# Moving the stores of a routing kernel from the sync engine's DMA queue to ScalarE's, almost a pair late

## The chip, the cores and the metric

The kernel runs on one core of one Trainium2 chip. The metric is device time in microseconds (us), lower is better. The core has a matrix engine (PE, with its weight loads listed apart as PEld), VectorE (DVE), ScalarE (ACT), GpSimd (POOL) and a sync engine (SP) that here does nothing but issue DMA transfers. A run's own median is quoted, and its ratio to the kernel before is the mean of its runs over the mean of the runs of the kernel before in the same rounds, so it is not quite the ratio of the two medians.

## The reference, cut to what matters

```python
B, S, D, H = 64, 1024, 1024, 16            # all fp32
best_head = np.argmax(x @ route_w, axis=-1)             # one head per token
for h in range(H):                                      # x split in 16 heads of 64
    out[:, :, h, :] = (x_heads[:, :, h, :] @ experts[h]) * (best_head == h)[:, :, None]
```

There are 65,536 tokens of 4 KB: 268 MB are read and 268 MB are written. The kernel works in tiles of 128 tokens, and in pairs of tiles: 256 pairs, each with 1 MB in and 1 MB out.

## The kernel before: the parts that matter

```python
WAYS = 2;  XIN_BUFS = 10;  OUT_BUFS = 6;  AHEAD = 7
ORDER = "TTTTFTFTFTTFTFTFTTTTTT"      # T: a transpose of the next pair, F: a whole block of this one

def load(g):                                           # one pair: two transfers of 512 KB
    xin = xin_pool.tile([P, 2, D], FP32, ...)
    for r in range(WAYS):
        nc.sync.dma_start(out=xin[r::WAYS], in_=xg[g, r::WAYS])      # 8 KB a partition
    return xin
...
def split_pass(xt):                                    # 20 small matmuls a tile, 64x64 weights
    for p in range(NS):
        for half in range(2):
            for th in range(2):
                nc.tensor.matmul(ps[...], lhsT=xt[...64 x 64...], rhs=mv[...64 x 80...], ...)
    nc.scalar.copy(out=raw[...], in_=ps[...])
...
for j in range(-2 * AHEAD, NT + 2, 2):                 # j: first tile of a pair
    if j + 2 * AHEAD < NT:
        xins[j + 2 * AHEAD] = load(j // 2 + AHEAD)
    ...
    for i in pair:                                     # the pair that was transposed last time
        work[i] = split_pass(xts[i])                   # a burst of 40 small matmuls (80 in the trace)
    for step in order:                                 # T: transpose (ScalarE copies every fourth)
        ...                                            # F: whole block; after three, finish()
        if f % NF == 0:                                # finish(): argmax, mask, products into ot
            finish(ot[:, i % 2, :], ps_w, *work.pop(i))
            if i == pair[1]:
                for r in range(WAYS):
                    nc.sync.dma_start(out=og[i // 2, r::WAYS], in_=ot[r::WAYS])
```

Loads and stores share one queue and stand in it in program order: two loads, two stores, two loads. In the trace a transfer is never issued before the one eight places earlier has landed (0.02 us after that landing at the earliest), so at most eight are in flight, and eight are in flight for 95% of the time.

## Time and profile before

| | |
|---|---|
| time, median of 3 | 1344.7 us (1339.88 to 1344.74) |
| profiled run, span | 1338.1 us |
| pair of tiles when nothing disturbs it | 4.93 us on PE |
| 256 such pairs | 1261 us |
| DMA busy share, 20 to 1300 us | 1.01 |

The page of the profile, cut to its span, busy times, DMA rows (40 equal slices: busy tenths, then GB/s), the data queue, the chain that ended last, and the DMA issues (KB each, median us from issue to landing):

```profile
span 1338.1 us, 66342 instructions
...
PE 1290.3 (96%) x27648; PEld 1208.3 (90%) x27648; DVE 933.7 (70%) x4098; ACT 923.2 (69%) x1537; POOL 721.9 (54%) x1031
...
DMA  8999999999999999999999999999999999999997
GB/s 340 421 421 416 413 407 409 407 407 406 412 398 377 418 417 399 395 412 414 398 393 404 410 416 418 402 408 397 410 407 410 412 407 417 416 405 416 417 409 327
...
q1 hardware_dynamic: 81920, 536.94, 98.6%
...
DMA 96%; PE 1%; SPq 0%; DVE 0%; issue 0%; POOL 0%; ACT 0%; ACTq 0%; POOLq 0%; DVEq 0%
DMA out_dram<-ot 95%; DMA xin<-in_x_dram 1%; SPq L106 0%; PE ps_w L150 0%; PE ps_t L115 0%; DMA mv<-in_route_w_dram 0%; PE ps_s L136 0%; POOL ot L181 0%; DVE ot L173 0%; ACTq L88 0%; ACT raw L143 0%; ACT xt L117 0%; DVE mask L164 0%; POOLq L249 0%; DVE lg L158 0%
...
xin<-in_x_dram SPq DMA_DIRECT2D x512, 512.0 KB, 10.2
out_dram<-ot SPq DMA_DIRECT2D x512, 512.0 KB, 10.2
```

Three things are to be seen. The DMA engines are full from the second slice to the last but one. The chain that ended last is stores. And a transfer lands 10.2 us after it is issued, because eight of 512 KB are nearly always in flight (4.2 MB at 408 GB/s are 10.3 us).

The waits list of the compute engines (who waited for whom: us in total, times, longest), cut to what touches DMA and PE:

```profile
DVE ot L173 <- DMA out_dram<-ot: 83.8, 104, 1.8
...
POOL ot L181 <- DMA out_dram<-ot: 76.3, 40, 3.0
...
PEld ps_s L136 <- issue: 62.8, 241, 1.9
...
PE ps_s L136 <- issue: 21.9, 35, 1.8
...
PE ps_t L115 <- DMA xin<-in_x_dram: 6.9, 2, 6.6
```

DVE and POOL wait 84 and 76 us for an output buffer that a store still reads.

From these views the kernel before is bound by the DMA engines, and the compute is held back through the output buffers.

### The profile page before, as it was taken

The page shows a single profiled execution, that of the slowest core. Times are in us where ns is not written, and L with a number is a line of the kernel's source. Part 1 is how long each engine was busy: PE and PEld are TensorE (multiplying, and loading weights), DVE is VectorE, ACT ScalarE, POOL GpSimd, SP SyncE. Part 2 cuts the span into 40 slices and gives each one's busy share as a digit, 9 for nine tenths or more (in the row PEclk, how much of TensorE's full clock was granted, in tenths as well). Part 3 has the DMA queues.
Part 4 walks back from the last instruction along what each step waited for, and adds up shares of the span by engine and source line. Part 5 has one row for each costly group of instructions (what it writes and reads, how often), then busy time and mean ns, then how long its engine had stood idle before and what let it go on. Part 6 is the DMA issues. An engine that isn't in the chain of part 4 may idle for free.

```text
span 1338.1 us, 66342 instructions
## 1 busy us (share of the span) xinstructions
PE 1290.3 (96%) x27648; PEld 1208.3 (90%) x27648; DVE 933.7 (70%) x4098; ACT 923.2 (69%) x1537; POOL 721.9 (54%) x1031
## 2 busy tenths in 40 slices
PE   7999999999999999999999999999999999999995
PEld 7888998999998999999998999889998999999995
DVE  4666766677776777777777677667777777767775
ACT  5666766767766777777676776667766767767673
POOL 3455555555555555555555555555555555555554
PEclk9999999999999999999999999999999999999998
DMA  8999999999999999999999999999999999999997
GB/s 340 421 421 416 413 407 409 407 407 406 412 398 377 418 417 399 395 412 414 398 393 404 410 416 418 402 408 397 410 407 410 412 407 417 416 405 416 417 409 327
DMA packets 84412, 541.51 MB, mean 405 GB/s; under 512 B 18576, under 2 KB 18576, under 8 KB 18576
## 3 DMA queue, kind: packets, MB, share of 16 engines
q1 hardware_dynamic: 81920, 536.94, 98.6%
q8 instruction: 218, 3.57, 1.0%
q10 hardware_dynamic: 2192, 0.33, 0.1%
q14 instruction: 82, 0.67, 0.1%
HBM read 268.76 MB, written 268.44 MB: 401 GB/s over the span
## 4 chain that ended last, share of the span: by engine, by line
DMA 96%; PE 1%; SPq 0%; DVE 0%; issue 0%; POOL 0%; ACT 0%; ACTq 0%; POOLq 0%; DVEq 0%
DMA out_dram<-ot 95%; DMA xin<-in_x_dram 1%; SPq L106 0%; PE ps_w L150 0%; PE ps_t L115 0%; DMA mv<-in_route_w_dram 0%; PE ps_s L136 0%; POOL ot L181 0%; DVE ot L173 0%; ACTq L88 0%; ACT raw L143 0%; ACT xt L117 0%; DVE mask L164 0%; POOLq L249 0%; DVE lg L158 0%
## 5 line engine op out<-in xcount | busy, mean ns | idle before, releaser
L181 POOL TENSOR_TENSOR ot<-raw,mask 128x384 f32<-128x384 f32 (+1 forms) x1024 | 721.2, 725 | 605.6 <-ACT xt L117 338.0
L117 ACT COPY xt<-ps_t 128x512 f32<-128x512 f32 x1024 | 576.7, 589 | 288.5 <-PE ps_t L115 288.0
L115 PE MATMUL ps_t<-ident,xin 128*128 128x128 f32 x4096 | 756.5, 277 | 9.7 <-DMA xin<-in_x_dram 6.9
L150 PE MATMUL ps_w<-mf,xt 128*128 128x144 f32 x3072 | 580.3, 289 | 1.5 <-DVE ot L173 1.1
L115 PEld LDWEIGHTS ps_t<-ident,xin 128*128 128x128 f32 x4096 | 499.7, 141 | 33.6 <-issue 8.9
L150 PEld LDWEIGHTS ps_w<-mf,xt 128*128 128x128 f32 x3072 | 464.2, 191 | 8.8 <-DVE ot L173 6.3
L136 PE MATMUL ps_s<-mv,xt 64*64 64x80 f32 x20480 | 430.0, 232 | 22.6 <-issue 21.9
L136 PEld LDWEIGHTS ps_s<-mv,xt 64*64 64x64 f32 x20480 | 381.1, 133 | 73.2 <-issue 62.8
L143 ACT COPY raw<-ps_s 128x704 f32<-128x704 f32 x512 | 371.1, 747 | 104.3 <-PE ps_s L136 64.9
L173 DVE TENSOR_TENSOR ot<-ps_w,mask 128x384 f32<-128x384 f32 x512 | 285.6, 558 | 98.5 <-DMA out_dram<-ot 83.8
L127 DVE TENSOR_REDUCE lgs<-ps_s 128x16 f32<-128x96 f32 x512 | 121.4, 251 | 106.3 <-ACT raw L143 105.4
L164 DVE TENSOR_SCALAR mask<-hid,ix 128x16 f32<-128x16 f32 x512 | 120.0, 234 | 56.0 <-POOL ot L181 0.9
L124 DVE TENSOR_REDUCE lgw<-ps_w 128x16 f32<-128x48 f32 x512 | 103.3, 202 | 78.9 <-PE ps_w L150 78.1
L158 DVE TENSOR_TENSOR lg<-lgs,lgw 128x16 f32<-128x16 f32 x512 | 131.8, 257 | 17.6
L160 DVE MAX8 mx<-lg 128x8 f32<-128x16 f32 x512 | 91.2, 178 | 17.6
L162 DVE FIND_INDEX8 ix<-mx,lg 128x8 uint32<-128x16 f32 x512 | 86.5, 169 | 0.0
L162 DVE MATCH_VALUE_LOAD ix<-mx,lg 128x8 f32 x512 | 47.2, 92 | 17.7
L117 ACT ACT_TABLE_LOAD x1 | 1.3, 1283 | 7.3 <-DMA mf<-in_experts_dram 7.3
L81 DVE MEMSET mf<- 128x432 f32 x1 | 0.4, 418 | 0.9 <-PEq L238 0.9
masks.py:197 POOL MEMSET ident<- 128x128 f32 x1 | 0.2, 205 | 0.3 <-POOLq L238 0.3
masks.py:199 POOL TENSOR_SCALAR_AFFINE_SELECT ident<-ident 128x128 f32<-128x128 f32 x1 | 0.3, 294 | 0.0
L238 POOL MEMSET const-float32-0.0<- 128x1 f32 x1 | 0.1, 99 | 0.2 <-issue 0.2
(5 smaller groups left out, 0.6 us busy)
## 6 DMA issues: line engine op xcount, KB each, us to landing
xin<-in_x_dram SPq DMA_DIRECT2D x512, 512.0 KB, 10.2
out_dram<-ot SPq DMA_DIRECT2D x512, 512.0 KB, 10.2
mv<-in_experts_dram ACTq DMA_DIRECT2D x2, 48.0 KB, 4.7
mf<-in_experts_dram ACTq DMA_DIRECT2D x2, 48.0 KB, 2.4
mv<-in_experts_dram ACTq DMA_DIRECT2D x2, 32.0 KB, 3.9
mv<-in_route_w_dram ACTq DMA_DIRECT2D x1, 24.0 KB, 4.6
mf<-in_route_w_dram ACTq DMA_DIRECT2D x1, 24.0 KB, 3.1
mv<-in_route_w_dram ACTq DMA_DIRECT2D x1, 16.0 KB, 3.2
```

Source lines behind the costliest of these rows:

```text
L115: nc.tensor.transpose(ps_t[:, q, :], xin[:, t, p * P:(p + 1) * P], ident)
L117: nc.scalar.copy(out=xt[:, half * (NB // 2):(half + 1) * (NB // 2), :], in_=ps_t)
L124: nc.vector.tensor_reduce(out=lg, in_=parts.rearrange("k s h -> k h s"), op=ALU.add, axis=AX.X)
L127: nc.vector.tensor_reduce(out=lg, in_=parts.rearrange("k b s h -> k h b s"), op=ALU.add, axis=AX.XY)
L136: nc.tensor.matmul(ps[th * 64:(th + 1) * 64, half, o0:o0 + W], lhsT=xt[half * 64:(half + 1) * 64, p, th * 64:(th + 1) * 64], rhs=mv[half * ...
L143: nc.scalar.copy(out=raw[:, :, 0:RW], in_=ps[:, :, 0:RW])
L150: nc.tensor.matmul(ps[:, o0:o0 + STEP], lhsT=xt[:, NS + f, :], rhs=mf[:, f, :], start=(f == 0), stop=(f == NF - 1), skip_group_check=True)
L158: nc.vector.tensor_add(out=lg, in0=lgs, in1=lgw)
L162: nc.vector.max_index(out=ix, in_max=mx, in_values=lg)
L164: nc.vector.tensor_scalar(out=mask, in0=hid, scalar1=ix[:, 0:1], scalar2=None, op0=ALU.is_equal)
L173: nc.vector.tensor_tensor(out=ov[:, NS:], in1=bc(mk[:, NS:]), op=ALU.mult, in0=ps[:, W:W + NF * STEP].rearrange("k (f w) -> k f w", w=STEP ...
L181: nc.gpsimd.tensor_tensor(out=ov[:, ab:NS:2], in0=rv4[:, 0:n, :, o0:o0 + Dh], in1=bc(mk[:, ab:NS:2]), op=ALU.mult)
```

## The change

The intent: loads should not stand behind stores whose data is not ready. Stores go to ScalarE's queue. Since a wait on that queue also holds up ScalarE's copies (by 1313.6 us in a run below), a store is placed almost a pair later, where its data should be ready; a seventh output buffer pays for that.

```diff
-OUT_BUFS = 6
+OUT_BUFS = 7
...
+    done = []
+    def store():
+        while done:
+            g, ot = done.pop(0)
+            for r in range(WAYS):
+                nc.scalar.dma_start(out=og[g, r::WAYS], in_=ot[r::WAYS])
...
-        for step in order:
+        for n, step in enumerate(order):
+            if n == 13:
+                store()
...
                 if i == pair[1]:
-                    for r in range(WAYS):
-                        nc.sync.dma_start(out=og[i // 2, r::WAYS], in_=ot[r::WAYS])
+                    done.append((i // 2, ot))
+    store()
```

## The prediction

> **What bounds the kernel now.** The 16 DMA engines. The page's DMA row is at 9 in all but the end slices; the one queue for loads and stores (q1: 81920 packets, 536.94 MB) takes 98.6% of 16 engines' span, and the windows view gives a DMA share of 1.00 to 1.02 from 20 to 1320 us. The chain that ended last is 95% `out_dram<-ot`. PE is a close second: undisturbed pairs start 4.93 us apart (timeline, first split matmuls), so 256 pairs would need about 1261 us, some 1285 with start and tail. The wait list shows how the DMA throttles the compute: VectorE and GpSimd wait 83.8 and 76.3 us for `ot` to come free; PE waits for a load only at the start (6.9 us).
>
> The packet records say what DMA can at best: a typical 8 KB packet takes 309 ns. 65,536 of them over 16 engines are 1266 us, the 4-byte completion writes about 10, instruction fetches about 15. The remaining 44 us or so are packets longer than 309 ns.
>
> **What the change does.** Work is the same: same bytes, packets, matmuls, copies. It moves 512 issues (0.50 us each on the sync queue, so about 1.0 us a pair) to ScalarE's sequencer. ScalarE is busy 923 of 1338 us, 3.6 of 4.93 us a pair, and idles 0.65 us just where the stores now stand, after the second transpose copy; by then the pair's GpSimd product has ended about 0.5 us earlier. So the issue itself fits. The instruction order shows each queue now holds at most four transfers in flight (each waits for the one four earlier in its own queue) in place of eight in one queue. Landing takes 10.2 us now, two pair periods, so stores will sometimes block ScalarE, and this, rather than the seven `ot` buffers, becomes the throttle of the compute. Loads no longer stand behind stores, and run ahead until the ten `xin` buffers are full.
>
> **How much is critical.** No bandwidth is gained: [...]the DMA share of 1.01 leaves nothing to fill. Two things can cost:
> 1. Mixing. [...]Today loads and stores come in blocks of two transfers; the long packets cluster where one kind follows the other (mean excess 15 to 18 ns a packet in the first half of a load block, 3 to 5 in its second transfer). If mixed traffic costs 14 to 17 ns everywhere, the 44 us become 57 to 70: +13 to +26 us (estimate).
> 2. Tail. Loads run further ahead, so more pairs are left to compute when only stores remain, at half the DMA demand: 0 to +10 us (estimate; now 24.6 us follow the last load's landing).
> Against that, loads that never wait behind a store may absorb some jitter: 0 to -12 us.
>
> **Prediction.** 1356 us (+0.8%); 1325 to 1392 holds it 8 times in 10. Faster by over 2%: 0.08; within 2%: 0.62; slower: 0.30.
>
> **What would show it.** DMA share still about 1.0 through the middle; mean GB/s per slice 395 to 405; median landing still near 10 us on both queues; the wait on `ot` buffers (160 us) mostly gone, replaced by ScalarE's queue waiting for `out_dram<-ot`; PE idle longer, waiting for ScalarE's copies; last load issued earlier than 1303 us.
>
> **What would make it wrong.** [...]If blocked stores hold ScalarE so long that both queues run dry, the DMA share falls below 0.97 and it is slower by 3% or more. If mixing costs far more than at today's transitions, likewise.

## More of the kernel before

A matmul of the program appears as two in the trace: a pair has 108 matmuls and 108 weight loads there, 80 of each in the burst.

The waits of the sync engine's queue:

```profile
SPq L223 <- DMA out_dram<-ot: 373.2, 469, 1.7
SPq L106 <- DMA xin<-in_x_dram: 335.6, 496, 2.0
```

The queue spends its time waiting for transfers to land, not for compute.

PE waits for a load only at the start. What PE does wait for is called "issue": nothing that the profile shows.

## The result, and the profile after

| | before | after |
|---|---|---|
| median | 1344.7 us | 1381.45 us (1381.3 to 1382.48, 3 runs) |
| ratio | | 1.0288, 95% interval 1.0252 to 1.0323 |
| span of the profiled run | 1338.1 us | 1379.4 us |

The change makes the kernel 2.9% slower. A second series later (below) gave 1387.24 us and a ratio of 1.0346. The prediction was 0.8% slower, so its range held the time but its size was too small by more than a factor of three.

The page after, the same parts:

```profile
span 1379.4 us, 66341 instructions
...
PE 1299.7 (94%) x27648; PEld 1216.3 (88%) x27648; DVE 928.6 (67%) x4098; ACT 920.7 (67%) x1537; POOL 720.5 (52%) x1031
...
DMA  8999999999999999999999999999999999999975
GB/s 320 402 418 416 415 395 402 395 399 399 416 392 391 394 401 387 400 394 393 398 413 403 399 403 401 403 416 402 403 397 399 411 403 413 408 401 397 395 294 215
...
q1 hardware_dynamic: 40960, 268.47, 49.7%
q10 hardware_dynamic: 43152, 268.80, 47.4%
...
PE 89%; DMA 4%; issue 4%; ACTq 1%; ACT 1%; DVE 1%; POOL 0%; POOLq 0%; SPq 0%; DVEq 0%
PE ps_t L115 34%; PE ps_s L136 29%; PE ps_w L150 26%; DMA xin<-in_x_dram 3%; ACTq L198 1%; ACT xt L117 1%; DMA out_dram<-ot 1%; DMA mv<-in_experts_dram 0%; DVE ot L173 0%; DVE lg L158 0%; ACT raw L143 0%; DMA mf<-in_experts_dram 0%; DVE lgw L124 0%; DVE ix L162 0%; DVE mx L160 0%
...
xin<-in_x_dram SPq DMA_DIRECT2D x512, 512.0 KB, 7.7
out_dram<-ot ACTq DMA_DIRECT2D x512, 512.0 KB, 7.0
```

The chain that ended last is now PE (89%), not stores. Landing takes 7.7 and 7.0 us in place of 10.2, so the queues are no longer always full (two to four transfers in flight on the loads' queue from 100 to 1300 us, at most four on the stores'), and yet the DMA row is still at 9 until the last two slices. A busy share of 1.00 with 402 GB/s is a poor guide here: it counts the time that packets took, and packets took longer here (by how much is given under "Mixing" below). The tell-tale is who waits for whom. The sync queue after:

```profile
SPq L106 <- PE ps_t L115: 726.5, 238, 4.8
SPq L106 <- DMA xin<-in_x_dram: 114.4, 137, 3.8
```

Loads wait for PE to free an input buffer. Before, they waited for transfers. The compute engines after:

```profile
PEld ps_s L136 <- issue: 99.5, 322, 1.6
...
PE ps_s L136 <- issue: 45.4, 64, 1.4
PEld ps_s L136 <- ACT xt L117: 16.7, 19, 3.8
...
PE ps_s L136 <- ACT xt L117: 13.4, 12, 3.6
...
PE ps_t L115 <- DMA xin<-in_x_dram: 7.5, 2, 6.7
```

The waits for output buffers are gone, as intended. In their place PE and its weight loads wait more for "issue": 45.4 us where it was 21.9, and 99.5 where it was 62.8. One such wait, in the timeline of PE (start us, us, what, how many, and in brackets the idle time before it):

```profile
start us, us, engine line op out<-in xcount [idle before <-releaser]
585.80 0.64 PE L136 MATMUL ps_s<-mv,xt 64*64 64x80 f32 x23
587.72 0.91 PE L136 MATMUL ps_s<-mv,xt 64*64 64x80 f32 x37 [1.28 <-issue]
```

PE stops for 1.28 us in the middle of the burst of small matmuls, where all its data is there and no semaphore is awaited.

The trace holds each DMA packet too, so these stops can be laid beside them. Queue q8, "instruction", carried 218 packets of 16 KB in either kernel. PE executes 27,648 matmuls and as many weight loads, 55,296 instructions, and 55,818 with those of its sequencer; 218 packets for them are one packet for every 256, so q8 is evidently PE's own instruction stream. Our own count of all stops of PE and PEld together of over 0.06 us, by the number of the PE instruction after the stop:

```
                         before           after            after, second trace
at every 256th           24.8 us in 49    49.2 us in 76    55.5 us in 77
anywhere else             1.2 us in  5    13.8 us in 15    15.4 us in 17
```

Nearly every stop in the steady state falls exactly 256 instructions, or a multiple, after the one before it, and PE resumes 1.2 to 1.7 us after an instruction packet has ended. Not every fetch stops PE: of some 217 boundaries between blocks of 256 instructions 49 show a stop before and 76 after. The burst issues 160 instructions in 1.6 us, the rest of the pair 56 in 3.3 us, and a fetch that comes late in the burst stops PE.

The stops elsewhere, 14 us, are mostly before 80 us, up to 3.6 us long (4.7 us in the second trace), where ScalarE's sequencer stands at a store until an earlier transfer has landed (the stores beside the five longest are issued 0.02 to 0.10 us after a landing, three times that of an earlier store, twice that of a load). The gap between the two stores of a pair is over 0.1 us only 7 times in the whole run, 12.3 us in all.

The stops can also be laid against the pairs (our own count: 255 pairs, each from the first small matmul of its burst to that of the next):

```
                                   before       after        after, second trace
pairs without a stop of PE         203          167          163
  their time over 4.93 us, in sum  10.2 us      4.6 us       4.9 us
pairs with a stop                  52           88           92
  their time over 4.93 us, in sum  43.2 us      95.2 us      103.0 us
```

Pairs without a stop keep the undisturbed pace in both kernels, so two issues a pair on ScalarE and the waits for output buffers cost PE next to nothing there. All that the changed kernel loses between its first and last pair it loses in pairs with a stop, 1.5 us for each us of stop counted (1.65 before). And the kernel before was limited nearly as much by PE and its stops as by the DMA engines (making PE's work cheaper gains it 1.3%, below): the output buffers hold PE back by some 10 us at most in the pairs without a stop.

Last, the windows view before and after (busy us and instruction count of PE, PEld, DVE, ACT, POOL; then granted clock, DMA share, GB/s), with the last stretch beginning about where the last load has landed (after) or shortly before (before):

```profile
core 0: us, PE busy (x) PEld busy (x) DVE busy (x) ACT busy (x) POOL busy (x), PEclk, DMA share, GB/s
20.00:100.00 80.00, 75.17 (x1618) 70.36 (x1617) 54.11 (x239) 54.10 (x90) 42.26 (x60) 1.00 1.01 418
100.00:1300.00 1200.00, 1178.82 (x25299) 1104.63 (x25301) 853.91 (x3750) 843.63 (x1407) 659.18 (x936) 1.00 1.01 408
1300.00:1338.00 38.00, 23.57 (x524) 21.58 (x518) 20.78 (x88) 16.39 (x28) 16.89 (x24) 0.85 0.81 333
```

```profile
20.00:100.00 80.00, 68.15 (x1311) 63.48 (x1309) 45.22 (x199) 43.87 (x74) 34.04 (x49) 0.91 1.00 401
100.00:1300.00 1200.00, 1149.94 (x24624) 1076.74 (x24623) 826.02 (x3649) 818.75 (x1368) 640.66 (x912) 1.00 1.00 402
1320.00:1379.00 59.00, 49.34 (x1075) 46.20 (x1073) 38.80 (x172) 34.82 (x59) 30.93 (x44) 0.96 0.57 233
```

In the tail of the changed kernel the DMA engines are little over half used for 59 us: the last load lands 6 us into this stretch, when the bursts of eight pairs are still to start (two in the kernel before), and then only stores move. The time from the last load's landing to the end is 24.6 us before and 53.2 us after.

### The profile page after: what moved, and what is told of

Same layout as the page of the kernel before. It is cut to its first block, busy times and chain, and to the rows that moved or that the text cites. A ratio compares the mean times of both kernels' runs of the same rounds, so it can differ in the third digit from the quotient of the medians.

```text
span 1379.4 us, 66341 instructions
## 1 busy us (share of the span) xinstructions
PE 1299.7 (94%) x27648; PEld 1216.3 (88%) x27648; DVE 928.6 (67%) x4098; ACT 920.7 (67%) x1537; POOL 720.5 (52%) x1031
## 4 chain that ended last, share of the span: by engine, by line
PE 89%; DMA 4%; issue 4%; ACTq 1%; ACT 1%; DVE 1%; POOL 0%; POOLq 0%; SPq 0%; DVEq 0%
PE ps_t L115 34%; PE ps_s L136 29%; PE ps_w L150 26%; DMA xin<-in_x_dram 3%; ACTq L198 1%; ACT xt L117 1%; DMA out_dram<-ot 1%; DMA mv<-in_experts_dram 0%; DVE ot L173 0%; DVE lg L158 0%; ACT raw L143 0%; DMA mf<-in_experts_dram 0%; DVE lgw L124 0%; DVE ix L162 0%; DVE mx L160 0%
## 5 line engine op out<-in xcount | busy, mean ns | idle before, releaser
L136 PE MATMUL ps_s<-mv,xt 64*64 64x80 f32 x20480 | 444.2, 233 | 60.2 <-issue 45.4
L136 PEld LDWEIGHTS ps_s<-mv,xt 64*64 64x64 f32 x20480 | 387.6, 133 | 118.2 <-issue 99.5
L127 DVE TENSOR_REDUCE lgs<-ps_s 128x16 f32<-128x96 f32 x512 | 129.2, 253 | 197.3 <-ACT raw L143 196.4
L158 DVE TENSOR_TENSOR lg<-lgs,lgw 128x16 f32<-128x16 f32 x512 | 112.2, 219 | 17.6
```

The lines of the kernel that those rows point to most:

```text
L127: nc.vector.tensor_reduce(out=lg, in_=parts.rearrange("k b s h -> k h b s"), op=ALU.add, axis=AX.XY)
L136: nc.tensor.matmul(ps[th * 64:(th + 1) * 64, half, o0:o0 + W], lhsT=xt[half * 64:(half + 1) * 64, p, th * 64:(th + 1) * 64], rhs=mv[half * ...
L158: nc.vector.tensor_add(out=lg, in0=lgs, in1=lgw)
```

## The experiments

Four theories were on the table.

- **Run-ahead.** Freed from the stores, loads run ten pairs ahead; at the end ten pairs of compute are left beside a half-used DMA.
- **Mixing.** Loads and stores on two queues are mixed more, which makes packets longer (guess: in what order an engine takes the packets of two queues, no trace here shows). The part of packet time over the usual 309 ns rose from 45 us (summed, divided by 16 engines) to 62 us (69 in the second trace). This part is called the excess below.
- **Instruction fetch.** PE has become the limit, because its fetches come late.
- **ScalarE.** The issue work or the waits on its queue hold up its copies.

"Fetch stalls" below are PE's stops at every 256th instruction, counted as above. All ratios are to the kernel before on the same chip.

### Which part of the change does it

**Late stores on the old queue**: the change with one line back.

```diff
-                nc.scalar.dma_start(out=og[g, r::WAYS], in_=ot[r::WAYS])
+                nc.sync.dma_start(out=og[g, r::WAYS], in_=ot[r::WAYS])
```

> The whole change except the queue: stores half a pair late, seven out buffers, but still on the sync queue. If the queue is what costs, this is the time of the kernel before, 1340 us (within 0.7%): loads still stand behind stores, last load lands near 1313 us, packet excess over 309 ns near 45 us, PE fetch stalls near 25 us. If the lateness itself costs (stores start later, tail longer), it is 1350 us or more.

Measured: 1341.54 us, ratio 1.0028 (0.9985 to 1.007). Fetch stalls 21.1 us, excess 42 us. The lateness and the seventh buffer cost nothing; the queue does.

**Stores on ScalarE's queue at once**, without the lateness.

```diff
-            if n == 13:
-                store()
...
                     done.append((i // 2, ot))
+                    store()
```

> The queue move without the lateness: stores on ScalarE's queue right after the pair is finished. If the loads' run-ahead is the cause, the tail stays (about 53 us from last load landed to end) and the time is at least that of the change, 1380 us. If ScalarE being held up by the issue matters, this is clearly worse than the change, because ScalarE's queue waits there for GpSimd's product (1400 us or more, ScalarE copies seen as releaser of PE waits).

Measured: 2664.48 us, ratio 1.9882 (1.9792 to 1.9972). Worse than any theory had said. Its waits list:

```profile
POOL ot L181 <- ACT xt L117: 1708.6, 248, 8.8
ACT xt L117 <- issue: 1313.6, 255, 6.1
DVE lgs L127 <- ACT raw L143: 1174.5, 512, 12.1
```

ScalarE idles 1313.6 us for "issue", its queue standing at the store until the pair is finished, while GpSimd and VectorE wait for ScalarE's copies, and a pair takes 10.36 us in place of 4.93 (medians). So the late placement is not decoration: without it this change costs a factor of two. It says nothing yet on the 2.9%.

### Run-ahead

**Six input buffers in place of ten, in the changed kernel.**

```diff
-XIN_BUFS = 10
+XIN_BUFS = 6
-AHEAD = 7
+AHEAD = 5
```

> The changed kernel with six input buffers in place of ten, so that loads can run at most six pairs ahead. Run-ahead theory: last load lands later relative to the end, tail shrinks from 53 to about 33 us, and the time falls by some 10 us (half of the 20 us, since the DMA engines are half used in the tail), to about 1370 us. Instruction-fetch theory[...]: PE stalls after fetches stay at 54 us and the time stays at 1380 us within 0.3%.

Measured: 1374.23 us, ratio 1.0262 (1.0214 to 1.031). The tail fell from 53.2 to 33.4 us, as forecast. Fetch stalls stayed at 49.4 us. The time lies between the two forecasts: by the ratios 0.3% below the first series of the changed kernel and 0.8% below the second (given below), with overlapping intervals in both cases. The first traces differ by 4.8 us, and a count by pairs finds all of it in the pairs with a stop (95.2 us before this edit, 90.0 with it). A cost of the longer tail is not shown here.

**Loads ten pairs ahead with twelve buffers, in the kernel before** (XIN_BUFS 12, AHEAD 10).

> The kernel before, one queue, with loads ten pairs ahead in program order and twelve input buffers. Run-ahead theory: the tail grows from 25 us by about 3 pairs of compute, to 35 to 40 us, and the time by 4 to 8 us, with packet excess and fetch stalls as before (45 and 25 us). Fetch or mixing theory: no change, 1340 us within 0.3%.

Measured: 1337.19 us, ratio 1.0000 (0.9953 to 1.0047). The tail grew to 34.6 us, as the theory said, but the time did not move: in that tail the DMA share was 0.73, as in the kernel before (0.72), so that more stores must have been left to drain. Here a longer tail cost nothing as long as the DMA share in it stayed the same.

### Is the compute slower by itself

**Only half of the stores** (even rows only; wrong result), in either kernel.

```diff
-            for r in range(WAYS):
+            for r in range(1):
```

> The changed kernel storing only the even rows (wrong result on purpose): a quarter of the bytes less, compute unchanged. This shows the compute's own floor. If DMA load alone delays the compute, about 1290 us with fetch stalls under 10 us; if being on ScalarE's queue costs the compute in itself, it stays above 1310 us.

> The kernel before storing only the even rows (wrong result on purpose): the control for the run above. About 1285 to 1290 us, bound by PE (256 pairs of 4.93 us plus start and tail).

Measured: 1310.1 us for the changed kernel (ratio 0.9769, 0.9742 to 0.9797) and 1313.14 us for the kernel before (0.982, 0.9777 to 0.9863), both higher than expected. With a quarter of the bytes gone the two are alike, so issuing 256 transfers (one a pair) from ScalarE costs the compute nothing by itself. Both chains that ended last are PE, 97 and 98%. Fetch stalls were 19.0 and 12.5 us: they shrink with the load on the DMA engines, but do not vanish.

### Spreading the burst: a failed experiment

The 40 small matmuls of a pair were cut into ten groups of four, between transposes and whole blocks, in both kernels.

```diff
-ORDER = "TTTTFTFTFTTFTFTFTTTTTT"
+ORDER = "TTTTFSTSFSTSFSTTFTFTFTATATATATAT"    # S, A: four small matmuls of this pair's second, next pair's first tile
```

> The changed kernel with the 40 small split matmuls of a pair (80 matmul and 80 weight-load instructions in one burst of 1.6 us) spread over the whole pair in groups of four between transposes and whole blocks. Same work, same queues. Instruction-fetch theory[...]: the stalls that end 1.3 to 1.5 us after a fetch fall from 54 us to under 15, and the time falls by 25 us or more, to 1355 us or less. Mixing theory ([...]the DMA engines bound the kernel): packet excess stays at 60 us or more and the time stays within 10 us of 1380.

> The same spreading in the kernel before. Both theories have it bound by the DMA engines, which are already full: 1340 us within 1%, fetch stalls falling from 25 us to under 10. If it is faster by over 1%, fetch stalls were critical there too.

Measured: 2079.25 us (ratio 1.5518) and 2085.11 us (1.5558), both theories missed. A pair takes 8.05 us in place of 4.93. Nine more groups are 18 more changes between the small matmuls and the others, and (8.05 - 4.93) / 18 is 0.17 us each, an estimate that puts the whole growth on the changes. The fetch stalls did fall, to 0.2 us in both, but with the DMA engines 70% used that proves little. The test does not tell the theories apart.

### Two queues, both kinds on each

Both queues carry both kinds, in the old order: even rows on the sync queue, odd rows on ScalarE's.

```diff
-        for r in range(WAYS):
-            nc.sync.dma_start(out=xin[r::WAYS], in_=xg[g, r::WAYS])
+        nc.sync.dma_start(out=xin[0::WAYS], in_=xg[g, 0::WAYS])
+        todo.append((g, xin))        # odd rows: from ScalarE's queue, in store()
...
-                nc.scalar.dma_start(out=og[g, r::WAYS], in_=ot[r::WAYS])
+            nc.sync.dma_start(out=og[g, 0::WAYS], in_=ot[0::WAYS])
+            nc.scalar.dma_start(out=og[g, 1::WAYS], in_=ot[1::WAYS])
```

> Two data queues that both carry loads and stores in the old order (even rows on the sync queue, odd rows on ScalarE's), so two queues are busy[...] and loads can't run ahead of stores. Instruction-fetch theory:[...] stalls at every 256th instruction stay at 40 us or more and the time is 1365 us or more. Mixing theory: excess near 45 us and about 1345 us. Run-ahead theory: short tail (25 us) and about 1345 us.

Measured: 1410.5 us, ratio 1.0506 (1.047 to 1.0542). Fetch stalls 46.4 us, stops elsewhere 25.1 us (ScalarE is held up more, since its queue now waits for loads too), tail 42.4 us, excess 91 us. The fetch theory's forecast (40 us or more, 1365 us or more) held. Mixing had forecast 1345 us and an excess near 45; it fails on both, though the extra hold-ups of ScalarE keep this from being a clean test.

### Packet size

**4 KB packets**: each transfer takes one row of a pair from all 128 partitions in place of both rows from 64.

```diff
-            nc.sync.dma_start(out=xin[r::WAYS], in_=xg[g, r::WAYS])
+            nc.sync.dma_start(out=xin[:, r], in_=xg[g, :, r])      # stores alike
```

> The changed kernel with each transfer split by row of the pair in place of partition parity: still two transfers of 512 KB a load and a store, but packets of 4 KB in place of 8 KB[...]. Instruction-fetch theory: PE's stalls at every 256th instruction fall from 49 us to 35 us or less and the time falls by 10 us or more, to 1370 us or less. Mixing or run-ahead theory: the time stays at 1380 us or rises (more packets[...]).

> The same 4 KB packets in the kernel before, one queue. It is held back by the DMA engines, so shorter fetch waits gain little: within 1% of 1340 us, stalls at every 256th instruction falling from 25 us to under 20; a small loss if short packets carry the DMA engines less well.

Measured: 1412.19 us (ratio 1.0544, 1.0498 to 1.0591) and 1370.44 us (1.0208, 1.0164 to 1.0252). Both were missed in direction: fetch stalls rose to 80.3 and 59.8 us. The idea that shorter packets help the fetch is not borne out.

**16 KB packets**: tiles of two pairs, transfers still 512 KB and two loads and two stores a pair.

```diff
-WAYS = 2;  XIN_BUFS = 10;  AHEAD = 7;  (g p t) with t=2
+WAYS = 4;  XIN_BUFS = 5;   AHEAD = 6;  (g p t) with t=4;  OUT_BUFS = 4
```

> The changed kernel with tiles of two pairs, so that each DMA packet is 16 KB in place of 8 KB; transfers stay 512 KB, two loads and two stores a pair, stores on ScalarE's queue. The 4 KB runs showed that more packets delay PE's instruction fetch. Instruction-fetch theory, in that form: half as many packets, so the fetch starts earlier (mean delay from 3.7 to about 3.3 us), PE's stalls at every 256th instruction fall from 49 us to 35 us or less, and the time to 1360 us or less. DMA theory (the packets' own cost bounds it; 159 ns for 4 KB and 309 ns for 8 KB give 609 ns for 16 KB, 1.5% less): stalls unchanged, about 1360 us too, but then the time no longer follows 1285 us plus 1.45 times PE's idle gaps, which held for the compute-bound runs within 6 us.

> The kernel before with 16 KB packets, one queue. It is held back by the DMA engines, so it gains what the packets gain, about 1.5%: 1318 to 1328 us, and would be the fastest of all. If PE's stalls fall under 20 us it may come near the 1311 us of the half-stored runs. Miss if 1335 us or more.

Measured: 1424.44 us (ratio 1.0632, 1.06 to 1.0664) and 1393.62 us (1.0428, 1.0386 to 1.047), missed again: fetch stalls 66.2 and 72.8 us. The one-queue run is the instructive one: one queue, loads and stores in the old order, only coarser (a store waits for two pairs to be done, and there is room for eight pairs of output in place of six). Its chain, its sync queue and PE's waits:

```profile
PE 92%; issue 5%; ACTq 1%; DVE 0%; DMA 0%; ACT 0%; POOL 0%; POOLq 0%; DVEq 0%
```

```profile
SPq L198 <- DVE ot L174: 314.5, 128, 6.3
...
SPq L108 <- DMA xin<-in_x_dram: 8.8, 13, 1.7
```

```profile
PEld ps_s L137 <- issue: 115.4, 334, 2.0
...
PE ps_s L137 <- issue: 64.4, 80, 1.9
```

It is bound by PE, its queue waits for the compute and hardly ever for a load to land, and PE waits for "issue" even more than in the changed kernel. So a second queue is not necessary for the slowdown: one queue does the same as soon as the fetch stalls are this long. And the time of a PE-bound run follows PE's stops. The line given in advance, 1285 us plus 1.45 times the stops (an estimate fitted to the earlier runs), with the stops at 256 and elsewhere together:

| run | stops, us | line, us | span of the profiled run, us |
|---|---|---|---|
| stores on ScalarE, six input buffers | 60.1 | 1372 | 1374.6 |
| changed kernel, first trace | 63.0 | 1376 | 1379.4 |
| changed kernel, second trace | 70.9 | 1388 | 1387.4 |
| 4 KB packets, one queue | 61.9 | 1375 | 1374.6 |
| 16 KB packets, one queue | 72.8 | 1391 | 1390.0 |
| 4 KB packets, two queues | 91.0 | 1417 | 1413.0 |
| 16 KB packets, two queues | 84.5 | 1408 | 1416.0 |
| both kinds on both queues | 71.5 | 1389 | 1410.0 |
| half of the stores, one queue | 12.5 | 1303 | 1311.2 |
| half of the stores, two queues | 19.0 | 1313 | 1310.5 |

Only the second trace of the changed kernel and the 16 KB rows came after the line was written down; of these the two-queue 16 KB run is 8 us off, as is the half-stored one-queue run of the rows before. The row of both kinds on both queues is 21 us off, and it is not bound by PE alone (its chain that ended last has 67% PE and 21% DMA). The kernel before has 26.0 us of stops, for which the line gives 1323 us, under its 1338: there the DMA engines come first.

**Transfers of 256 KB in the kernel before** (WAYS 4: 2 MB in flight in place of 4).

> The kernel before with four transfers of 256 KB a load and a store, so that eight transfers in flight are 2 MB in place of 4 MB; packets stay 8 KB, one queue. If the fetch waits behind all the bytes that are queued, its mean delay falls from 3.1 us to about 2 us and the stalls from 25 us to under 15[...]. Time within 1% of 1340 us either way.

Measured: 1577.95 us, ratio 1.1759 (1.17 to 1.1819), far outside what was expected: with 2 MB in flight and 1,024 more issues the queue moved 345 GB/s. The fetch delay, measured from the 190th instruction of a block to the start of the next instruction packet (a fixed mark, not the true request), did fall from a mean of 3.1 to 2.1 us and the fetch stalls to 4.1 us. With half the bytes in flight the delay was a third shorter, as forecast; what the fetch waits for is not shown. The compute was held back so much that the time says no more.

### Taking PE's limit away

The small matmuls read only the upper half of each fp32, as bf16 (wrong result). Queues, transfers and copies stay; PE has 136 instructions a pair in place of 216, and a small matmul takes 204 ns in place of 229 (medians, stores on ScalarE).

```diff
-                        lhsT=xt[half * 64:(half + 1) * 64, p, th * 64:(th + 1) * 64],
-                        rhs=mv[half * 64:(half + 1) * 64, p, :],
+                        lhsT=xt[half * 64:(half + 1) * 64, p, th * 64:(th + 1) * 64].bitcast(BF16)[:, 1::2],
+                        rhs=mv[half * 64:(half + 1) * 64, p, :].bitcast(BF16)[:, 1::2],
```

> The changed kernel with the split matmuls reading only the upper half of each fp32 (a bf16 view; wrong result on purpose): same queues, transfers and copies, but PE has half the instructions in the burst[...]. Instruction-fetch theory: with PE and its fetches out of the way the two queues carry as much as one, so the time is that of the DMA engines, within 1% of the run below (1325 to 1350 us), and PE's stalls at every 256th instruction no longer matter. DMA theory (two queues carry less[...]): it stays at 1370 us or more.

> The same cheaper split matmuls in the kernel before (wrong result on purpose), the control. It is held back by the DMA engines already, so it gains little: 1325 to 1342 us. A gain of over 2% would mean that PE was critical there too.

Measured: 1348.45 us with the stores on ScalarE (ratio 1.0053, 1.0011 to 1.0095) and 1322.67 us with one queue (0.987, 0.9835 to 0.9905). The two-queue kernel fell by 33 us, the one-queue kernel by 16 to 22 (medians of different series). The range of 1325 to 1350 us held for the first, but not "within 1% of the run below": they are 1.9% apart. The control fell 2 us under its range. Fetch stalls are 0.8 us in both. The middle of the two runs, two queues first (columns as above, the last two being DMA share and GB/s):

```profile
100.00:1280.00 1180.00, 988.62 (x15706) 881.67 (x15704) 856.51 (x3697) 796.71 (x1386) 650.72 (x925) 1.00 1.01 413
```

```profile
100.00:1280.00 1180.00, 1056.23 (x15693) 889.69 (x15691) 864.28 (x3687) 795.66 (x1384) 647.11 (x921) 1.00 1.01 412
```

With PE out of the way two queues carry 413 GB/s and one carries 412. The excess of the packets is 36 and 35 us. Loads and stores stand on the same two queues in the first of these runs as in the changed kernel, so this alone does not make packets longer. (The trace of two queues is of one of the two fastest of six executions, 1338 us; the four at 1348 to 1350 us left none.) Long packets go along with queues that run low: the half-stored runs, with a quarter less traffic, have an excess of 147 us (stores on ScalarE) and 160 us (one queue). We read them as a sign of DMA engines short of work more than a cost. And the two-queue kernel is mainly bound by DMA again, as its chain and its sync queue show, though its loads still wait 414 us for buffers that PE frees:

```profile
DMA 90%; PE 5%; ACT 2%; ACTq 1%; issue 1%; DVE 0%; POOL 0%; POOLq 0%; SPq 0%; DVEq 0%
```

```profile
SPq L107 <- DMA xin<-in_x_dram: 633.3, 477, 3.8
SPq L107 <- PE ps_s L137: 414.1, 234, 4.2
```

What is left between these two is 26 us of median time, 14.5 us between the profiled runs. Their tails differ: 46.6 us at a DMA share of 0.57 against 24.2 us at 0.72. Idle DMA in the tail is thus 46.6 x 0.43 = 20 us against 24.2 x 0.28 = 7 us.

**The same with six input buffers** tests that.

> The changed kernel with cheap split matmuls (wrong result on purpose) and, besides, six input buffers in place of ten. If what is left between a_bf (1348 us) and b_bf (1323 us) is the loads' run-ahead, the tail after the last load landed falls from 47 to about 27 us and the time by 8 to 15 us, to 1333 to 1340 us. If two queues cost something else, it stays within 4 us of 1348.

Measured: 1336.61 us, ratio 0.9973 (0.9936 to 1.0011), tail 28.0 us: 12 us faster by the medians, as expected. So once the DMA engines are the limit, run-ahead seems to cost 12 us of the 26; the two intervals only just touch. But the two profiled executions took the same time (spans of 1336.4 and 1336.9 us), so no trace shows where the gain comes from. The other 14 us stay open.

**The changed kernel once more.**

> The changed kernel itself once more, beside the run above: a second trace of it, to see how far the stalls at every 256th PE instruction (49 us in the first) and the time (1381 us) repeat. 1376 to 1386 us and 44 to 56 us of stalls.

Measured: 1387.24 us, ratio 1.0346 (1.0305 to 1.0386), fetch stalls 55.5 us: a little slower than expected, with stalls at the top of the range.

No version beat the kernel before with a right result. The one with twelve input buffers and the late one on the old queue equal it.

## Why the prediction was wrong

- **"What bounds the kernel now. The 16 DMA engines" held only in part.** The sync queue waits for transfers, and making PE cheaper gains only 1.3%. But PE was level with them, not 50 us behind: with a quarter of the bytes gone it still takes 1311 us, not 1285, and in the kernel before itself 203 of 255 pairs ran undisturbed and the rest lost 43 us to PE's stops.
- **"So the issue itself fits" held.** With two issues of 0.48 us on ScalarE 167 pairs without a stop exceed 4.93 us by 4.6 us in sum, and the half-stored runs, with one issue a pair, are alike on both queues.
- **"Stores will sometimes block ScalarE, and this ... becomes the throttle of the compute" failed.** The gap between a pair's stores shows 12.3 us of such blocking, in 7 pairs. The throttle is PE.
- **"No bandwidth is gained" held**, and two queues lose none: 413 against 412 GB/s when PE asks for it.
- **"Mixing ... +13 to +26 us" failed as a cause**, although the symptom came in as forecast (excess up by 18 us); that it did is chance. The run with cheap matmuls, with the same two queues, has an excess of 36 us. The clustering of long packets where loads and stores meet, on which this term rested, was evidently not a cost that grows with mixing.
- **"Tail ... 0 to +10 us": the longer tail came (24.6 to 53.2 us), its cost is not shown.** In the changed kernel, which PE limits, six input buffers gain 0.3 to 0.8%, in the traces wholly in pairs with a stop; where DMA is the limit they gain 12 us by the medians.
- **The signs**: the wait on output buffers did vanish and the DMA share stayed at 1.0. Landing "near 10 us" was wrong (7.7 and 7.0), and that is the sign that the queues were no longer the limit. "Last load issued earlier than 1303 us" was wrong (1317). "PE idle longer, waiting for ScalarE's copies" was half right: longer, but mostly for its own instructions.

The step that failed is the list under "How much is critical": it named two costs, both on the DMA side, and let PE stay at its undisturbed 4.93 us a pair ("some 1285 with start and tail"). The instruction fetches were entered only as 15 us of DMA time. What the runs showed in that place: between the first and the last pair (every fourth copy of transposes on ScalarE) the mean pair rose from 5.136 to 5.317 us, which over 255 pairs is 46 us. Pairs without a stop kept 4.93 us; those with a stop went from 52 to 88, and their excess from 43 to 95 us. The stops themselves grew by 24 us at the fetches (31 in the second trace) and 13 elsewhere; the remaining 9 us are time in which PE is recorded as busy (gaps under 0.06 us come to 0.2 us at most in either trace). With PE relieved, the two-queue kernel is level with the kernel before (1.0053), but still 1.8% slower than one queue with the same relief: only between a third and a half of the loss of 2.9 to 3.5% goes. That the forecast had the sign right is luck: the cost that was measured is not among those it added up.

What stays open: why the fetches of the kernel before stop PE only 25 us while two queues, 4 KB packets or 16 KB packets for the same bytes stop it for 46 to 80 us. It is not the number of queues alone (one-queue runs have it too) and not the packet size in one direction. One reading would be that a kernel throttled by its output buffers gives the fetches time. The traces speak against it: the pairs without a stop run equally fast, and it is the fetch that comes later. Counted from PE's passing a block boundary, the next instruction packet starts after 2.86 us on average before and 2.90 us with late stores on the old queue, but after 3.20 and 3.24 us in the changed kernel and 3.14 and 3.26 us with 4 and 16 KB packets on one queue. How the instruction queue is served among the data queues is not visible in these traces.

## What to carry to other kernels

When PE and the DMA engines are both above nine tenths, work out before moving a queue how long the compute's own path is with its stops, not only with undisturbed pairs. Here a PE wait on "issue" that recurs every 256 instructions was a late instruction fetch, and with PE's work as it is, the stops were longer beside fuller DMA engines: 12.5 and 19.0 us at a share of 0.88, 21 to 80 us at about 1.00 (an exception is the run with 256 KB transfers, otherwise held back: 4.1 us at 0.95). Judge which side binds by what the issuing queue waits for (transfers landing, or buffers freed by compute), by the time to landing, and by how many pairs run undisturbed, not by the busy share of the DMA engines, which was 1.00 and 1.01 here. A queue that a compute engine also works from must have its stores placed where the data is ready: here a placement too early doubled the time.
